# RMSNorm with SiLU on one core: other piece sizes in the first storing phase, and one alignment directive less

## The chip, the core and the metric

The kernel runs on one core of a Trainium2 chip. The core has engines that run side by side, each with its own list of instructions: VectorE (DVE in the profile), ScalarE (ACT), GpSimd (POOL), SyncE (SP) and TensorE (PE, unused here). Sixteen DMA engines move data between the memory of the chip (HBM) and the core's buffer SBUF. The metric is the device time of one execution in microseconds; lower is better.

## The reference

```python
x: 16 x 1024 x 512 float32; gamma: 512; eps
rms = np.sqrt(np.mean(x ** 2, axis=-1, keepdims=True) + eps)
x_norm = x / rms * gamma
return x_norm * (1.0 / (1.0 + np.exp(-x_norm)))
```

There are 16,384 rows of 512 elements. Each row is divided by the root of its mean square, multiplied by gamma, and passed through SiLU. Every byte is read once (33.55 MB) and written once (33.55 MB).

## The kernel before

**Tiles.** The 16,384 rows are spread over 128 partitions, so a partition has 128 rows. When this text says "row n" it means one row of every partition, 128 x 2 KB = 256 KB. The rows are cut into six groups in DRAM (L28), and inside a group each partition's rows are contiguous, so that a load or store of n rows is one run of n x 2 KB per partition. SBUF holds a ring of 96 rows (`xb`, L29): row 96 goes where row 0 was, and so on.

**Chunks.** The computation goes in 32 chunks of 4 rows (`cn`, L37). For chunk k, ScalarE squares the four rows; two of them are summed by its accumulator (L181) and two go to PSUM (L188), where VectorE adds them up (L234). GpSimd adds eps (L162) and raises to the power -0.5 (L169). VectorE multiplies each row by its factor and by gamma in place (L245). ScalarE applies SiLU in place (L200), two chunks behind its squares (L223 to L230).

**Loads.** SyncE issues all ten loads in order (L30, L31, function `load`, L118 to L127). The first two are placed in the entry block, ahead of the start barrier (L142 to L151). The first seven, rows 0 to 95, fill the ring and wait for nothing. Each of the last three, (96,16), (112,12) and (124,4), overwrites a part of the ring and so waits for each store that reads that part (`over`, L121); in addition the table `behind` (L35) lets (96,16) wait for one store more. A semaphore that SyncE has waited for once is not waited for again. SyncE does nothing between these waits, so a load behind a waiting load waits too.

**Stores.** ScalarE issues the eight stores (L32, L33, `store`, L206 to L212) in its own instruction list, between its squares and SiLUs. A store waits for the SiLU of its last chunk. The table `hold` (L34) keeps all stores back until chunk 12 and until load (64,28) has landed, and store (32,32) until chunk 22 and until load (112,12) has landed. Work on the DMA engines therefore falls into four phases: loading rows 0 to 95, storing rows 0 to 31 (the first storing phase), loading rows 96 to 127, and storing rows 32 to 127. The first storing phase has three stores, (0,16), (16,12) and (28,4), and ScalarE issues them one after the other.

**Semaphores.** Each DMA has a semaphore of its own, `ld[i]` or `st[u]`. Each of the 16 DMA engines adds one to it when its share is done; the waiting engine goes on at 16, that is, when the last DMA engine is done.

**Alignment.** For ScalarE, VectorE and GpSimd an `addr_align` is put ahead of the first instruction of the entry block (L131 to L141). It makes that engine's list begin at a chosen slot, counted within blocks of 128 instructions: slot 8, 40 and 0. It computes nothing. Instructions reach an engine through DMA transfers of their own, which the profile shows as queue q14. Loads are queue q1 and stores are queue q10. A list without the directive begins wherever the loader puts it.

Of the kernel before, what the change touches and what calls it, by code (L numbers as in the profile page):

```python
# [9 lines left out]
def kernel(  # L10
# [7 lines left out]
    nc = tc.nc  # L18
# [10 lines left out]
    ring = 96  # L29
    loads = [(0, 4), (4, 4), (8, 8), (16, 16), (32, 32), (64, 28)]  # L30
    loads += [(92, 4), (96, 16), (112, 12), (124, 4)]  # L31
    stores = [(0, 16), (16, 12), (28, 4), (32, 32), (64, 32)]  # L32
    stores += [(96, 16), (112, 8), (120, 8)]  # L33
    hold = {0: ((64, 28), 12), 3: ((112, 12), 22)}  # L34
    behind = {(96, 16): (16, 12)}  # L35
    early = 2
    cn = 4  # L37
    n_sq = 2
# [13 lines left out]
    behind = {loads.index(a): stores.index(b) for a, b in behind.items()}  # L52
# [78 lines left out]
    for queue, engine, offset in (  # L131
        (nc.scalar, mybir.EngineType.Activation, 8),
        (nc.vector, mybir.EngineType.DVE, 40),
        (nc.gpsimd, mybir.EngineType.Pool, 0),
    ):
        ins = queue.addr_align(128, offset=offset, max_nops=0).ins
        assert here[-1] is ins or here[-1].name == ins.name
        here.pop()
        entry.insert(
            next(i for i, other in enumerate(entry) if other.engine == engine), ins  # L140
        )  # L141
# [161 lines left out]
```

## Time and profile before

| what | value |
|---|---|
| median of 3 runs | 160.28 us (160.19 to 160.35) |
| the profiled execution: its own time | 160.17 us |
| the profiled execution: its span, first to last instruction | 159.3 us |
| VectorE busy | 124.4 us (78%) |
| ScalarE busy | 129.7 us (81%) |
| GpSimd busy | 65.4 us (41%) |
| HBM read and written | 33.56 MB and 33.56 MB, 421 GB/s over the span |

The span is what the trace covers; 0.9 us of the execution's own time lie around it. The page gives busy time by engine, then the span in 40 slices of 4 us. A digit is the busy share in tenths, and the DMA row is the mean over the 16 DMA engines. A view of one stretch of time counts packets: a packet is one contiguous run moved by one DMA engine, here mostly the rows of one partition in one load or store (8, 16, 24 or 32 KB and more), or the 4-byte increment of a semaphore. These views book a packet's bytes and busy time where the packet begins, so a share over a short stretch can exceed 100%. The trace also holds the start, length, queue and size of each packet.

### The profile page before, as it was taken

Reading aid. Unit: us, or ns where it says so; the run is one execution under the profiler, and the core shown is the slowest. Engines: PE = TensorE matmul, PEld = TensorE weight load, DVE = VectorE, ACT = ScalarE, POOL = GpSimd, SP = SyncE. Lnnn points to the kernel's source line nnn. Section 1 sums busy time; section 2 is a strip of 40 time slices with the busy share of each in tenths; the row PEclk is TensorE's granted clock in tenths of the full one; section 3 lists DMA queues with packets and bytes.
Section 4 is the critical chain, followed back from the end, with each engine's and each line's share of the span. In section 5 each row is a group of like instructions: output and inputs, shape, how many; then the busy total and the mean of one; then the engine's idle time right before and its main releaser. Section 6 shows DMA issues by size and latency. Waiting matters only on the chain.

```text
span 159.3 us, 503 instructions
## 1 busy us (share of the span) xinstructions
DVE 124.4 (78%) x162; ACT 129.7 (81%) x193; POOL 65.4 (41%) x71
## 2 busy tenths in 40 slices
DVE  0049996999289999599999999999999999992000
ACT  0675979997499995999999999999999999945000
POOL 1035553555145555155555555555555555540000
DMA  7999997998999969999899898969969969999997
GB/s 251 448 467 407 411 593 329 510 444 362 461 432 446 461 280 446 477 399 426 370 397 411 387 469 379 609 280 510 527 263 527 527 263 527 395 395 395 440 420 325
DMA packets 2750, 67.17 MB, mean 422 GB/s; under 512 B 437, under 2 KB 437, under 8 KB 441
## 3 DMA queue, kind: packets, MB, share of 16 engines
q1 hardware_dynamic: 1440, 33.56, 49.7%
q10 hardware_dynamic: 1304, 33.57, 49.0%
q14 instruction: 6, 0.04, 0.1%
HBM read 33.56 MB, written 33.56 MB: 421 GB/s over the span
## 4 chain that ended last, share of the span: by engine, by line
ACT 57%; DMA 25%; DVE 4%; issue 3%; ACTq 1%; SPq 0%
ACT xb L200 25%; DMA xb<-in_x_dram 25%; ACT junk L181 18%; ACT sq L188 14%; DVE xb L245 3%; ACTq L210 1%; DVE ms L234 1%; SPq L125 0%; ACTq L178 0%
## 5 line engine op out<-in xcount | busy, mean ns | idle before, releaser
L245 DVE SCALAR_TENSOR_TENSOR xb<-xb,rstd,gamma_sb 128x512 f32<-128x512 f32 x128 | 87.3, 744 | 0.0
L200 ACT ACTIVATE xb<-xb 128x2048 f32<-128x2048 f32 x32 | 60.9, 1903 | 5.0 <-DVE xb L245 3.4
L234 DVE TENSOR_REDUCE ms<-sq 128x2 f32<-128x1024 f32 x32 | 39.2, 1223 | 19.0 <-ACT sq L188 16.0
L162 POOL TENSOR_SCALAR aeps<-ms 128x4 f32<-128x4 f32 x32 | 20.6, 644 | 71.6 <-DVE ms L234 71.6
L169 POOL TENSOR_TENSOR rstd<-aeps,neg_half 128x4 f32<-128x4 f32 x32 | 44.0, 1376 | 2.7
L181 ACT ACTIVATE junk<-xb 128x512 f32<-128x512 f32 x64 | 37.2, 582 | 6.3 <-DMA xb<-in_x_dram 6.3
L188 ACT ACTIVATE sq<-xb 128x1024 f32<-128x1024 f32 x32 | 32.1, 1005 | 0.0
L181 ACT ACTIVATION_READ_ACCUMULATOR junk<-xb 128x1 f32 x64 | 11.9, 186 | 0.0
L221 ACT ACT_TABLE_LOAD x1 | 1.3, 1283 | 5.4 <-issue 5.4
L258 DVE LOAD_MASK_SELECT gamma_sb<-gamma x1 | 0.0, 14 | 1.1 <-DMA gamma<-in_gamma_dram 1.1
L258 DVE STREAM_SHUFFLE gamma_sb<-gamma 128x512 f32<-128x512 f32 x1 | 0.7, 716 | 0.0
L156 POOL MEMSET blank<- 128x16 f32 x1 | 0.1, 111 | 1.1 <-POOLq L66 1.1
L157 POOL MEMSET gamma<- 128x512 f32 x1 | 0.5, 524 | 0.0
L284 POOL MEMSET const-float32-0.0<- 128x1 f32 x1 | 0.1, 98 | 0.7 <-issue 0.7
L284 POOL MEMSET const-bfloat16-1.0<- 128x1 bf16 x1 | 0.1, 101 | 0.0
L284 POOL MEMSET const-uint8-127<- 128x1 uint8 x1 | 0.1, 101 | 0.0
L158 POOL MEMSET neg_half<- 128x4 f32 x1 | 0.1, 101 | 0.0
L284 POOL MEMSET const-float32-1.0<- 128x1 f32 x1 | 0.1, 99 | 0.0
## 6 DMA issues: line engine op xcount, KB each, us to landing
xb<-in_x_dram SPq DMA_DIRECT2D x2, 4096.0 KB, 16.3
out_dram<-xb ACTq DMA_DIRECT2D x2, 4096.0 KB, 15.3
xb<-in_x_dram SPq DMA_DIRECT2D x1, 7168.0 KB, 55.8
xb<-in_x_dram SPq DMA_DIRECT2D x4, 1024.0 KB, 13.6
out_dram<-xb ACTq DMA_DIRECT2D x2, 2048.0 KB, 13.7
out_dram<-xb ACTq DMA_DIRECT2D x1, 3072.0 KB, 19.6
xb<-in_x_dram SPq DMA_DIRECT2D x1, 3072.0 KB, 19.0
xb<-in_x_dram SPq DMA_DIRECT2D x1, 2048.0 KB, 11.1
```

The source lines that it names most:

```text
L157: nc.gpsimd.memset(gamma4, 0.0).then_inc(s_zero, 1)
L162: nc.gpsimd.tensor_scalar(out=aeps[:, k, :], in0=ms[:, k, :], scalar1=eps_f, scalar2=None, op0=ALU.add,),
L169: nc.gpsimd.tensor_tensor(out=rstd[:, k, :], in0=aeps[:, k, :], in1=neg_half, op=ALU.pow),
L181: acc = nc.scalar.activation(out=junk[n % 2], in_=xb[:, at + j, :], func=AF.Square, scale=inv_d**0.5, accum_out=ms[:, k, j : j + 1],)
L188: square = nc.scalar.activation(out=sq[k % 2], in_=xb[:, at : at + n_sq, :], func=AF.Square, scale=inv_d**0.5,)
L200: nc.scalar.activation(out=rows, in_=rows, func=AF.Silu), s_norm, k + 1
L210: nc.scalar.dma_start(out=dram(of, stores[t]), in_=buf(stores[t])),
L221: nc.scalar.preload_act_table_set("silu_and_others")
L234: nc.vector.tensor_reduce(out=ms[:, k, 0:n_sq], in_=sq[k % 2], op=ALU.add, axis=mybir.AxisListType.X,),
L245: ins = nc.vector.scalar_tensor_tensor(out=row, in0=row, scalar=rstd[:, k, j : j + 1], in1=gamma_sb, op0=ALU.mult, op1=ALU.mult,)
L258: nc.vector.stream_shuffle(gamma_sb, gamma4, [0] * 32), s_gld, 16
L284: nc = _bacc.Bacc("TRN2", target_bir_lowering=False, num_devices=1)
```

## The change

The first storing phase is cut into 16, 8 and 8 rows in place of 16, 12 and 4, and `behind` names the second of these, so that load (96,16) waits for stores (0,16) and (16,8). Load (112,12) goes into ring rows 16 to 27, which are now read by stores (16,8) and (24,8): SyncE waits for the third store ahead of this load, where it waited for the third store only ahead of load (124,4). ScalarE issues the three stores at the same place as before. GpSimd's list loses the alignment directive, and with it one instruction of its entry block; the lists of ScalarE and VectorE keep theirs and keep their lengths.

```diff
-    stores = [(0, 16), (16, 12), (28, 4), (32, 32), (64, 32)]
+    stores = [(0, 16), (16, 8), (24, 8), (32, 32), (64, 32)]
     stores += [(96, 16), (112, 8), (120, 8)]
     hold = {0: ((64, 28), 12), 3: ((112, 12), 22)}
-    behind = {(96, 16): (16, 12)}
+    behind = {(96, 16): (16, 8)}
...
     for queue, engine, offset in (
         (nc.scalar, mybir.EngineType.Activation, 8),
         (nc.vector, mybir.EngineType.DVE, 40),
-        (nc.gpsimd, mybir.EngineType.Pool, 0),
     ):
```

## The prediction

> **What bounds the kernel now.** I read the page first. Loads and stores together keep the 16 DMA engines busy for nearly the whole span:
>
> ```profile
> span 159.3 us, 503 instructions
> ...
> q1 hardware_dynamic: 1440, 33.56, 49.7%
> q10 hardware_dynamic: 1304, 33.57, 49.0%
> q14 instruction: 6, 0.04, 0.1%
> ```
>
> 49.7% and 49.0% make 98.7%, so about 2 us are lost per DMA engine, of which the packet list puts the first 1.0 us ahead of the first packet. VectorE (78%) and ScalarE (81%) have room. After the last SiLU at 146.4 us the stores already queued run on to 158.8 us, so the end is the end of the slowest DMA engine, and ScalarE's 57% in the chain is work beside full queues. The question is what each DMA engine loses at the change of phase. SyncE's waits name it:
>
> ```profile
> SPq L123 <- DMA out_dram<-xb: 74.8, 1, 74.8
> SPq L125 <- DMA out_dram<-xb: 1.3, 1, 1.3
> ```
>
> The 74.8 us are the wait before load (96,16); the 1.3 us are the wait for store (28,4) before load (124,4). The timeline of SyncE shows when the wait ended:
>
> ```profile
> 79.22 2.65 SPq L125 DMA_DIRECT2D xb<-in_x_dram  x3
> ```
>
> Store (16,12) landed at 79.13 us, the load was issued at 79.22 and its first packets begin at 80.18: 1.05 us from landing to packet. The DMA view of 79.72 to 80.16 us shows the hole between:
>
> ```profile
> DMA packets 6, 0.02 MB, mean 56 GB/s; under 512 B 3, under 2 KB 3, under 8 KB 3
> ...
> q10 hardware_dynamic: 6, 0.02, 13.5%
> ```
>
> Three data packets begin there and no load packet. By the packet list 11 of the 16 engines finish store (28,4) at 79.55 to 79.68 us, two at 79.74 and 79.86, and three late ones at 80.02, 80.98 and 81.08.
>
> **Who is late, and why that matters.** The late engines carry instruction fetches. In 2.6 to 3.2 us:
>
> ```profile
> q1 hardware_dynamic: 27, 0.22, 93.3%
> q14 instruction: 3, 0.02, 10.0%
> ```
>
> Each fetch takes 0.32 us, and the load packet behind it takes 0.68, 0.88 or 0.94 us in place of 0.31: three engines fall 0.7 to 0.95 us behind. One fetch more at 70.59 us (0.31, and the 24 KB packet behind it 1.37 for 0.91) and one at 78.64 (0.31, and 0.50 for 0.31) fall on two of these three. They are the engines that finish at 80.98 and 81.08.
>
> The hole costs a prompt engine about 0.6 us idle, plus a slow first load packet (1.69 to 2.21 us for 1.213). The two last engines lose nothing: their first load packets start at 80.98 and 81.08, take 1.24 and 1.21 us and end at 82.22 and 82.30. The prompt ones end theirs at 82.00 to **82.49**. So the hole levels the engines, and only 82.49 - 82.30 = **0.19 us** of it stands in the end time. The ends agree: all 16 finish within 158.30 to 158.77 us.
>
> **The change, part by part.**
>
> *Bytes and packets.* Before, an engine's share of rows 16 to 31 is 8 packets of 24 KB and 8 of 8 KB at steps of 0.908 and 0.305 us: 9.70 us. After, it is 16 of 16 KB at 0.607 us (steps of the last store): 9.71 us. The difference is 0. ScalarE issues three stores from 59.11 us as before: nothing.
>
> *Earlier release.* The engine last in store (16,12) begins it at 70.90 us and, with the fetch's 0.46 us, finishes at 78.62; landing is 0.5 us later. With 8 packets of 0.607 it finishes at 70.90 + 0.46 + 4.86 = 76.22, lands at 76.72, and loads begin at 77.77. Prompt engines begin store (24,8) at about 74.68 and end it at 79.54; the last two end it at 80.97 and 81.08 as now. Every engine then has a load queued before its stores run out: 1.8 us of cover on prompt engines (before: -0.6), 3.3 on the last. If no store packet is interleaved, prompt engines gain about 1.3 us each, but the last engine still begins its loads at 81.08. The end moves from the 82.49 group to the 82.30 engine: **-0.19 us**. Nothing later levels the engines again; prompt ones would end near 157.2.
>
> *The new wait.* Load (112,12) now waits for store (24,8), with (124,4) behind it on SyncE. A store that finishes at 81.08 lands at 81.6, and its load is on offer at 82.7, while (96,16) keeps the engines busy to 79.54 + 8 x 1.213 = 89.2 (prompt) and 90.8 (last). The cover is 6.5 us, so the cost is 0. If that cover went, each late microsecond would delay the end.
>
> *Interleaving.* No view of before shows 16 KB stores and 32 KB loads queued on one engine together. The nearest rows: ScalarE's scratch store (64-byte packets) is issued at 2.05 us and its first packet runs only at 5.65, behind loads, 2.7 us later than a store's usual 0.9 after issue would have it. From then on it alternates with load packets, one for one (5.6 to 6.6 us):
>
> ```profile
> q1 hardware_dynamic: 51, 0.41, 96.8%
> q10 hardware_dynamic: 47, 0.00, 3.2%
> ```
>
> Load packets keep their 0.31 us there, so one bound is 0 per alternation. The other is the extra on a packet behind a fetch, the only row where changing queues costs something: 0.19 to 0.63 us. Below nothing is excluded for a packet that already runs at 27 GB/s. I take 0: in the scratch row a newcomer waited for roughly eight packets of 8 KB, and prompt engines have only two or three store packets left at 77.77, the last five.
>
> The Trainium skill, "DMA: Bandwidth & Descriptors", section "Queues, rings and completion order", says that a DMA engine takes turns between queues, a packet each. That speaks against this change: by it the earlier load would take turns with store (24,8) and delay the semaphore on which load (112,12) now waits, which makes the first rival the forecast.
>
> *The directive.* GpSimd's list is 85 instructions with its entry block and 84 after. From slot 0 it stays within a block of 128; from an unknown slot it may cross a border, and a fetch then falls somewhere else. From the rows above a fetch costs one DMA engine 0.5 to 0.95 us, or gains as much where it goes. The last engines carry two fetches each; the third late one, 1.06 us ahead of the last, carries one. I take 0, since GpSimd's fetches presumably fall on that third engine. GpSimd's start has cover: the early loads occupy the queues to about 7 us, and SyncE passed the start barrier at 2.3.
>
> **Sum.** 160.17 - 0.19 = 159.98 us for the profiled execution. The median shown is 0.11 above it, so 160.28 - 0.19 = 160.09; I say **160.1 us**, own range 159.9 to 160.5.
>
> **Rivals.**
>
> *Slower: packets alternate and the new wait takes the place of the old.* At 78.04 the last engine has five store packets and the semaphore ahead. Taking turns with loads, it sends them after six loads: 78.04 + 5 x 0.607 + 6 x 1.213 = 88.35, landing 88.85, load (112,12) on offer at 89.9. Prompt engines are out of work at 78.32 + 2 x 0.607 + 8 x 1.213 = 89.24: the old hole again, ten microseconds later, levelling again at about the old cost. That alone is 0. Each of the 11 alternating packets that costs extra adds to the last engine: 0.19 each is 2.1 us, half of that 1.05, hence **161.3 us**, up to 162.4. It decides from 0.03 us per packet (0.33 us in all). For it: the strict alternation once scratch runs. Against it: no extra on the loads there. Chance 0.25.
>
> *Slower: a fetch of GpSimd falls late on an engine that is among the last.* Fetch 0.5 to 0.95 us, less what that engine had in hand: about **160.8 us**. For it: the start slot is unknown. Against it: the third engine has 1.06 us in hand when no levelling follows. Chance 0.10.
>
> *Faster: the last engines lose their lag.* If fetches move so that their lag shrinks to the third engine's, the end falls by 0.19 + 1.06 = 1.25, to about **159.0 us**. For it: lag is all that keeps the hole's 1.3 us from the end. Against it: VectorE's and ScalarE's lists keep slots and lengths. Chance 0.15.
>
> **How the numbers follow.** Forecast 0.50, rivals 0.25, 0.10, 0.15. A measurement here tells about 0.2% (0.32 us) from no change. Faster by more: the faster rival and the edge of the forecast, 0.15 + 0.05 = 0.20. Slower by more: most of the two slower rivals and the other edge, 0.31. Within: 0.49. The range reaches into both sides until about 2 in 10 are left out: 159.5 to 161.4.
>
> **What would show it.** Right: the SyncE wait ends near 76.8; no engine is idle between 77 and 82 us; the SyncE wait for store (24,8) ends by 83; final packets spread from about 157.2 to 158.6. Wrong: load and store packets mixed from 78 to 88 us with longer times, a SyncE wait near 88 and a new hole near 89.5 (first rival); a q14 packet after 85 us (second); two late engines less than 1 us behind (third).

## The result, and the profile after

The changed kernel takes 161.51 us (median of 9 runs, 160.78 to 161.96), the kernel before 160.22 us in the same comparison (160.15 to 160.44). The ratio is 1.0072, 95% interval 1.0059 to 1.0085: slower by 0.7% (the ratio is that of the means; the medians differ by 1.29 us). The forecast was 160.1 us in a range of 159.5 to 161.4; sign and size are both wrong, and the time lies just outside the range.

The page of the changed kernel, its span and its DMA queues (packets, MB, share of 16 engines):

```profile
span 160.2 us, 502 instructions
...
q10 hardware_dynamic: 1304, 33.57, 49.3%
q1 hardware_dynamic: 1440, 33.56, 49.0%
q14 instruction: 5, 0.04, 0.1%
```

The span grew by 0.9 us (159.28 to 160.21, unrounded). The execution's own time is 161.51 us, so 1.30 us lie outside the span, where 0.89 did before. Between the two profiled executions the loss of 1.34 us thus has two parts: 0.93 us inside the span and 0.41 us outside. They have different causes. The profiled execution is the median one. Two of the nine took only 160.78 and 160.81 us, with spans of 159.5 us: the loss inside the span is not there every time.

**Inside the span.** The release came as worked out. SyncE's waits in the changed kernel:

```profile
SPq L123 <- DMA out_dram<-xb: 72.2, 1, 72.2
SPq L125 <- DMA out_dram<-xb: 6.5, 1, 6.5
```

The first, ahead of load (96,16), is 2.6 us shorter than before and ends at 76.7 us; the second is the new wait for store (24,8). SyncE's timeline, from 70 and from 80 us on, shows when each ends:

```profile
76.73 7.61 SPq L125 DMA_DIRECT2D xb<-in_x_dram  x3
...
83.54 0.80 SPq L125 DMA_DIRECT2D xb<-in_x_dram  x2
```

Load (112,12) is issued at 83.54 us, 6 us before any DMA engine needs it. The new wait costs nothing.

The cost is in the first load packet of the DMA engine that is last. The DMA view of 81.04 to 81.24 us holds a single packet:

```profile
DMA packets 1, 0.03 MB, mean 164 GB/s; under 512 B 0, under 2 KB 0, under 8 KB 0
...
q1 hardware_dynamic: 1, 0.03, 67.2%
```

A packet's whole length is booked where it begins, so its length can be read from the share: 67.2% of 16 engines over 0.20 us is 2.15 us, for 32 KB. The same reading of the kernel before, 81.05 to 81.15 us, at the same place:

```profile
DMA packets 2, 0.03 MB, mean 328 GB/s; under 512 B 1, under 2 KB 1, under 8 KB 1
...
q1 hardware_dynamic: 1, 0.03, 75.8%
q10 hardware_dynamic: 1, 0.00, 0.6%
```

75.8% x 16 x 0.10 us = 1.21 us. The last engine begins its loads at the same moment in both kernels and pays 0.94 us more for the first packet in the new one. At the end of the changed kernel, this engine alone is still storing, from 158.78 to 159.8 us:

```profile
DMA packets 1, 0.02 MB, mean 16 GB/s; under 512 B 0, under 2 KB 0, under 8 KB 0
...
q10 hardware_dynamic: 1, 0.02, 3.7%
```

One data packet begins there (at 159.21 us, ending at 159.82); the other 15 engines end by 158.74. Before, all 16 ended within 158.30 to 158.77.

The packet lists give the sequence on an engine; I put a packet down to the engine whose packet before it ends within 10 ns of its start. S is a store packet, L a load packet, with start and length in us:

```
before, prompt   79.27 S 0.31 | idle 0.64   | 80.21 L 2.01 | 82.23 L 1.22
before, last     80.47 S 0.31 | 80.77 S 0.31 | 81.08 L 1.21 | 82.29 L 1.21
after, prompt    77.67 S 0.61 | 78.28 S 0.73 | 79.02 S 1.21 | 80.23 L 1.21 | 81.44 L 1.21
after, last      79.82 S 0.61 | 80.42 S 0.61 | 81.05 L 2.15 | 83.21 L 1.21
```

The hole is gone, but not its price. A prompt engine moves its last store packet at half rate (16 KB in 1.208 us for 0.61) and the one before it somewhat slowed, and loses about 0.7 us instead of 1.4. Across the idle stretch the rule cannot tell which load packet belongs to which engine, so the first row shows a typical pair. The last engine, which lost nothing before, loses 0.94. From 83.21 against 82.49 us before, a difference of 0.72, it is further behind at its end (1.05), mainly through the first packet of load (124,4), which took 0.67 us for 0.31. Landing after the last packet took 0.12 us less: 0.93.

What the prompt engines gain is taken back at the next change of phase, where store (32,32) is held until load (112,12) has landed on all engines. ScalarE's timeline in the changed kernel:

```profile
99.44 0.34 ACTq L209 DMA_DIRECT2D out_dram<-xb  x1
```

In the kernel before:

```profile
98.66 0.34 ACTq L210 DMA_DIRECT2D out_dram<-xb  x1
```

The last engine's lateness delays the issue by 0.78 us, and prompt engines, whose loads are done near 99.6 us, wait for it until 100.3.

**Outside the span.** GpSimd's first memset in the changed kernel:

```profile
0.23 0.10 POOL L283 MEMSET const-float32-0.0<- 128x1 f32 x1 [0.23 <-issue]
```

And in the kernel before:

```profile
0.66 0.10 POOL L284 MEMSET const-float32-0.0<- 128x1 f32 x1 [0.66 <-issue]
```

Without the directive it comes 0.43 us earlier, and the time outside the span is 0.41 us longer. First memset plus time outside is 1.55 us before and 1.53 after.

### The profile page after: what moved, and what is told of

Same layout as the page of the kernel before. It is cut to its first block, busy times and chain, and to the rows that moved or that the text cites. A ratio compares the mean times of both kernels' runs of the same rounds, so it can differ in the third digit from the quotient of the medians.

```text
span 160.2 us, 502 instructions
## 1 busy us (share of the span) xinstructions
DVE 124.4 (78%) x162; ACT 129.7 (81%) x193; POOL 65.4 (41%) x71
## 4 chain that ended last, share of the span: by engine, by line
ACT 57%; DMA 24%; DVE 4%; issue 3%; ACTq 2%; SPq 0%
ACT xb L199 25%; DMA xb<-in_x_dram 24%; ACT junk L180 18%; ACT sq L187 14%; DVE xb L244 3%; ACTq L209 2%; DVE ms L233 1%; SPq L125 0%; ACTq L177 0%
```

## Experiments

Each comparison has its own runs of the kernel before beside it; their medians moved from 160.18 to 160.46 us, so ratios within a comparison are what counts. "Outside" is the profiled execution's time less its span. Theory A is that there are two separate costs, the moment of the release and the directive; theory B that the directive alone explains the loss; theory C that the size of the pieces does.

### One half of the change at a time

Pieces and release only, directive kept:

```diff
-    stores = [(0, 16), (16, 12), (28, 4), (32, 32), (64, 32)]
+    stores = [(0, 16), (16, 8), (24, 8), (32, 32), (64, 32)]
-    behind = {(96, 16): (16, 12)}
+    behind = {(96, 16): (16, 8)}
```

> Pieces 16, 8, 8 with the earlier release, GpSimd's directive kept. Theory A (two separate costs): the pieces cost the 0.9 us that the span grew, because the DMA engine that was last pays about 0.9 us more on its first load packet; the directive costs the 0.4 us that grew outside the span. Then this is about 161.1 us, with 0.9 us outside the span as in the kernel before, and one DMA engine ends about 1 us after the others. Theory B (the directive alone): losing it moved GpSimd's instruction fetch to 80.3 us, and that disturbs the change of phase; then this is 160.0 to 160.3 us.

Measured: 161.15 us against 160.41, ratio 1.0041 (1.0027 to 1.0055). Span 160.27, outside 0.88 us; fetches at 70.7 and 78.6 us as before. The last engine's first load packet took 2.09 us, after 0.36 us idle, and ended at 83.55.

Directive only:

```diff
-        (nc.gpsimd, mybir.EngineType.Pool, 0),
```

> Pieces as before, only GpSimd's directive removed. Theory A: +0.4 us outside the span and nothing inside, 160.6 us, with GpSimd's fetch near 80 us on the third late DMA engine, whose lag has room. Theory B: 161.1 to 161.5 us, all of the loss, inside the span.

Measured: 160.69 us against 160.41, ratio 1.0014 (1.0005 to 1.0023). Span 159.44, outside 1.31 us. GpSimd's fetch is gone from the start (two q14 packets there instead of three) and comes at 80.0 us, on an engine that is not among the last, without a trace in the end time.

Both halves cost, each in its own place: B falls, and so does the idea that the fetch at 80 us disturbs the loads, as far as a run with the old release can tell. 0.74 and 0.28 us make 1.02, of the 1.29 measured together; the other 0.27 us are not accounted for, and the changed kernel alone spreads over 1.2 us (160.78 to 161.96).

### Is it the cut or the moment?

From here on GpSimd's directive is kept in every run.

Four pieces, released after 28 rows as before:

```diff
+    stores = [(0, 16), (16, 8), (24, 4), (28, 4), (32, 32), (64, 32)]
+    behind = {(96, 16): (24, 4)}
+    hold = {0: ((64, 28), 12), 4: ((112, 12), 22)}
```

> Four pieces of 16, 8, 4 and 4 rows, load (96,16) released by the third, so after 28 rows as in the kernel before and with 4 rows to cover it; directive kept. Theory A (what counts is how many rows are left when the loads come): no change, 160.1 to 160.4 us. Theory C (what counts is the size of the pieces or the number of stores): 161 us, as with 16, 8, 8.

Measured: 160.40 us against 160.41, ratio 0.9997 (0.9987 to 1.0007).

The last 4 rows in twice as many packets:

```diff
+    stores = [(0, 16), (16, 12), (28, 2), (30, 2), (32, 32), (64, 32)]
+    hold = {0: ((64, 28), 12), 4: ((112, 12), 22)}
```

> Pieces 16, 12, 2, 2, released after 28 rows as before: the bytes beside the loads are those of the kernel before, in twice as many packets (16 of 4 KB per DMA engine). If the number of queued store packets makes the last engine pay: 0.5 to 0.9 us more, 160.9 to 161.3 us. If the time of the release counts: 160.3 to 160.5 us.

Measured: 160.39 us against 160.46, ratio 1.0001 (0.9992 to 1.0010). The number of queued packets doesn't count at this moment of release.

Pieces 16, 8, 8, but released when the kernel before releases:

```diff
         stored_by_sync.add(u)
+        if i in behind:
+            nc.sync.wait_ge(s_sum, 17)
```

> Pieces 16, 8, 8 and the directive kept, but SyncE also waits, ahead of load (96,16), for VectorE's 17th reduction, which ends at 79.3 us: the loads are released when the kernel before releases them. Theory A (the time that the loads wait beside queued stores counts): back to 160.3 to 160.5 us, and the last DMA engine's first load packet takes 1.2 to 1.4 us. Theory C (the 8-row pieces count): 161.1 us as with pieces 16, 8, 8 alone.

Measured: 160.54 us against 160.46, ratio 1.0012 (1.0003 to 1.0021). SyncE went on at 79.67 us rather than near 79.3:

```profile
79.67 2.77 SPq L127 DMA_DIRECT2D xb<-in_x_dram  x3
```

The last engine's first load packet took 1.74 us, not the 1.2 to 1.4 expected. C falls: with the cut of the changed kernel and nearly the old release, 0.12% is left of the pieces' 0.41%, and the release was 0.4 us late.

Pieces 16, 8, 8, released at 78 us:

```diff
+            nc.sync.wait_ge(s_norm, 15)
```

> Pieces 16, 8, 8, directive kept, load (96,16) held until VectorE's 15th group of rows is done, at 78.0 us: the moment of release of pieces 16, 10, 6, with the cut of the changed kernel. Theory A (the moment of the release decides, and the last DMA engine pays 0.8 to 0.95 us more on its first load packet for any release well before 79 us): 161.1 to 161.4 us. Theory D (only a release at the landing of the second store pays): 160.4 us.

Measured: 161.61 us against 160.36, ratio 1.0073 (1.0054 to 1.0093). The release:

```profile
78.17 4.32 SPq L127 DMA_DIRECT2D xb<-in_x_dram  x3
```

This costs more than the release at 76.8 us. Theory D (only a release at the landing of the second store pays) falls.

Pieces 16, 10, 6:

```diff
+    stores = [(0, 16), (16, 10), (26, 6), (32, 32), (64, 32)]
+    behind = {(96, 16): (16, 10)}
```

> Pieces 16, 10, 6: loads released two rows later than in the changed kernel, two earlier than before; directive kept. Theory A: the loads come on offer near 78.9 us while the last DMA engine has about four 12 KB packets left; if the extra on its first load packet comes from any overlap of over a microsecond, the span grows by 0.9 again (161.1 us); if it grows with the overlap, by about half (160.6 us). Theory B: 160.0 to 160.3 us.

Measured: 161.40 us against 160.41, ratio 1.0055 (1.0036 to 1.0074). That is more than either form of theory A expected. Two late engines paid here: first load packets of 1.99 and 2.18 us, each begun 0.3 to 0.9 us after the engine's last store packet.

### The ends of the scale

No extra wait, released after 16 rows:

```diff
-    behind = {(96, 16): (16, 12)}
+    behind = {}
```

> Pieces 16, 12, 4 as before, no extra wait: load (96,16) is released by store (0,16) alone, with 16 rows of stores still queued; load (112,12) then waits for store (16,12). Theory A with a fixed price (each DMA engine pays 0.8 to 0.95 us once at the change of phase): 161.1 to 161.4 us. Theory A with a price per alternating packet: 162 us and more, since eight packets or more alternate. If the alternation holds back the stores on which (112,12) waits, there is a second hole as well, and the time is over 162.

Measured: 160.74 us against 160.46, ratio 1.0019 (1.0010 to 1.0028): cheaper than the releases at 76.8 and 78.2 us, which neither form of theory A had. The loads are issued at 72.10 us, but the first load packet runs only at 76.94. Around it a store packet of 24 KB is slowed on every engine (1.77 to 1.81 us for 0.91 on ten of them, 1.02 to 1.75 on the others), and stores and loads mix. Load (96,16) ends at 90.82 us on the last engine, earlier than before (90.96), but each engine has one to four packets of store (28,4) left when its part of this load is done, and they go between the later loads until 93.4 us. With these counted in, the engines have both pieces of work done between 90.31 and 91.25 us, against 90.54 to 90.96 before: the last one has lost 0.29 us of the 0.46 by which the span grew.

Released after all stores:

```diff
+    stores = [(0, 16), (16, 8), (24, 8), (32, 32), (64, 32)]
+    behind = {(96, 16): (24, 8)}
```

> Pieces 16, 8, 8, load (96,16) released by the third store, so with no store left: the hole at its full length, on every DMA engine. The last engine's stores end at 81.1, loads come on offer at 82.6 and the slow first packet ends near 84.8, against 82.5 in the kernel before: 162.5 us. If it is under 161.2, leaving the overlap out is the better choice and the forecast's price of the hole was wrong.

Measured: 162.64 us against 160.46, ratio 1.0141 (1.0127 to 1.0155). The hole at its full length costs 2.2 us; here the price of an idle stretch plus a slow first packet was worked out rightly.

Pieces 16, 13, 3:

```diff
+    stores = [(0, 16), (16, 13), (29, 3), (32, 32), (64, 32)]
+    behind = {(96, 16): (16, 13)}
```

> Pieces 16, 13, 3, directive kept: released about 0.45 us later than before, so that the loads come on offer about 0.45 us before the last DMA engine runs out. All engines' loads start 0.45 us later, the last engine's first packet is partly slow: 160.7 to 160.9 us. If 160.4 us or less, the release of the kernel before is not the best one.

Measured: 160.93 us against 160.24, ratio 1.0039 (1.0024 to 1.0054). The last engine's first load packet took 1.99 us, although its loads were on offer only about 0.25 us before its stores ran out.

Pieces 16, 11, 5:

```diff
+    stores = [(0, 16), (16, 11), (27, 5), (32, 32), (64, 32)]
+    behind = {(96, 16): (16, 11)}
```

> Pieces 16, 11, 5, directive kept: the release falls between that of 16, 10, 6 (78.2 us, +0.9 us) and of the kernel before (79.1 us). Loads come on offer about 1.4 us before the last DMA engine runs out of stores. If the price appears as soon as that lead is over about 1 us: 161.1 to 161.4 us. If it grows evenly with the lead: 160.7 us.

Measured: 160.34 us against 160.24, ratio 1.0008 (0.9986 to 1.0030), and neither expectation holds: ten times in two groups, four from 159.78 to 159.93 us and six from 160.28 to 161.12. In the profiled execution (160.76 us) two late engines began their loads at 81.02 and 81.21 us. The first took 1.21 us for its packet, the other 1.98.

Put in order of the moment when SyncE goes on:

| SyncE goes on, us | kernel | ratio to before |
|---|---|---|
| 72.1 | released after 16 rows | 1.0019 |
| 76.8 | 16, 8, 8 | 1.0041 |
| 78.2 | 16, 8, 8 held by a wait | 1.0073 |
| 78.3 | 16, 10, 6 | 1.0055 |
| 78.7 | 16, 11, 5 | 1.0008, two groups |
| 79.2 | before | 1 |
| 79.4 | 16, 8, 4, 4 and 16, 12, 2, 2 | 0.9997 and 1.0001 |
| 79.7 | 16, 8, 8 held by a wait | 1.0012 |
| 80.0 | 16, 13, 3 | 1.0039 |
| 81.8 | 16, 8, 8 after all stores | 1.0141 |

The packet lists of these profiles also answer how much the lead counts. By lead I mean the time from when the loads are on offer (0.96 us after SyncE goes on, as in the kernel before) until the engine's own stores end. The two engines that end their stores last, with the extra on the first load packet (its length less 1.21 us):

| kernel | second last engine: lead, extra, us | last engine: lead, extra, us |
|---|---|---|
| 16, 13, 3 | 0.08, 0.60 | 0.25, 0.78 |
| 16, 8, 8 held to 79.7 | 0.17, 0.82 | 0.55, 0.53 |
| 16, 8, 4, 4 | 0.73, 0.46 | 0.96, 0.12 |
| before, with two directives for GpSimd (further down) | 0.81, 0.35 | 0.91, 0.11 |
| before | 0.80, 0.03 | 0.90, 0 |
| 16, 11, 5 | 1.36, 0 | 1.54, 0.77 |
| 16, 8, 8 | 3.1, 0 | 3.3, 0.88, and 0.36 idle |
| changed kernel | 2.9, 0.04 | 3.3, 0.94 |

Up to a lead of about 0.9 us the extra falls, with scatter, from 0.6 to 0.8 us to almost nothing. Beyond it the last engine pays again, and the second last, with nearly the same lead, does not. These are single executions, so the lead alone does not decide.

### The two groups

Pieces 16, 11, 5 again, one execution:

> Pieces 16, 11, 5 once more, for a second profile. If its time is near 159.8 us, the last DMA engines' first load packets take 1.2 us and all engines end within 0.6 us; if it is near 161 us, at least one of them takes about 2 us and ends about 1 us after the others.

Measured: 161.42 us. The DMA view of 81.2 to 81.4 us shows the last engine's first load packet, 83.2% x 16 x 0.20 us = 2.66 us long:

```profile
DMA packets 1, 0.03 MB, mean 164 GB/s; under 512 B 0, under 2 KB 0, under 8 KB 0
...
q1 hardware_dynamic: 1, 0.03, 83.2%
```

The same pieces without ScalarE's directive, which moves its fetch from 78.6 to 47.1 and 126.7 us:

```diff
-        (nc.scalar, mybir.EngineType.Activation, 8),
```

> Pieces 16, 11, 5 and ScalarE's directive removed (GpSimd's kept), which takes ScalarE's fetch away from 78.6 us, so that one DMA engine less runs late. Pieces 16, 11, 5 gave times in two groups, 159.8 to 159.9 and 160.3 to 161.1 us. If each late engine by itself either pays the 0.8 to 0.9 us or not, fewer late engines give more executions near 159.8 us and a median under that of the kernel before: 159.9 us. If it is not the late engines: a median of 160.3 us and the same two groups.

Measured: 160.22 us against 160.18, ratio 1.0017 (0.9999 to 1.0036); ten times from 159.91 to 161.07. The spread stays and the median does not fall, so the gain hoped for from fewer late engines did not show. But the profiled execution took 159.92 us, at the low end, and here is its last engine, 81.0 to 81.1 us:

```profile
DMA packets 2, 0.03 MB, mean 328 GB/s; under 512 B 1, under 2 KB 1, under 8 KB 1
...
q1 hardware_dynamic: 1, 0.03, 75.8%
q10 hardware_dynamic: 1, 0.00, 0.6%
```

75.8% x 16 x 0.10 us = 1.21 us, no extra. Load (96,16) ends at 90.69 us on its last engine, against 92.38 in the profile of 161.42 us, and the spans differ by 1.5 us (159.03 and 160.53). So the forecast's picture, last engine unharmed and the end a little earlier than before, does occur. With pieces 16, 8, 8 it is not the usual case; the two short executions of the changed kernel, with spans of 159.5 us, come near it.

### Does the price need the lag?

ScalarE's and VectorE's lists begin at slot 0, so that their fetches come at 79.0 and 100 to 101.5 us:

```diff
-        (nc.scalar, mybir.EngineType.Activation, 8),
-        (nc.vector, mybir.EngineType.DVE, 40),
+        (nc.scalar, mybir.EngineType.Activation, 0),
+        (nc.vector, mybir.EngineType.DVE, 0),
```

> The kernel before with ScalarE's and VectorE's start slots moved from 8 and 40 to 0: their fetches at 78.6 and 70.6 us come later, to about 83 and 102 us, so that the last DMA engines are only 0.7 to 0.95 us behind at the change of phase. The hole then opens about 0.8 us earlier, but the two fetches fall on engines that nothing levels again: between 160.0 and 160.7 us. It is the base for the next run.

Measured: 160.75 us against 160.36, ratio 1.0034 (1.0013 to 1.0055), with a wide spread (160.41 to 161.87).

With pieces 16, 8, 8 as well:

> Pieces 16, 8, 8 with both start slots at 0, against the run before this one. If the last engine pays its 0.9 us however far it lags: 0.7 to 0.9 us over that run. If the price needs the lag of 1.5 us that the fetches give: within 0.2 us of that run.

Measured: 161.24 us against 160.36 for the kernel before, ratio 1.0057 (1.0036 to 1.0078), 160.66 to 161.82. That is 0.5 us over the run before it, between the two answers, and both kernels spread over more than a microsecond. No fetch came near 83 us, where one was expected; it came at 79.0. This pair decides nothing.

### What the directive is worth

ScalarE's directive removed, GpSimd's kept:

```diff
-        (nc.scalar, mybir.EngineType.Activation, 8),
```

> The kernel before without ScalarE's directive, GpSimd's kept. If the 0.4 us outside the span are tied to GpSimd's list, the time outside the span stays 0.9 us. If they are tied to any list that begins without the branch of its directive, it is 1.3 us. The span may change by up to 0.9 us, since ScalarE's fetches move.

Measured: 160.34 us against 160.36, ratio 0.9997 (0.9985 to 1.0008); outside 0.89 us. Of these two lists only GpSimd's matters for the time outside; VectorE's was not tried.

A second directive for GpSimd:

```diff
+        (nc.gpsimd, mybir.EngineType.Pool, 16),
         (nc.gpsimd, mybir.EngineType.Pool, 0),
```

> The kernel before with a second directive ahead of GpSimd's list (slot 0, then slot 16), so that GpSimd branches twice before its first memset. If the measured time begins with GpSimd's first instruction after the branch: the first memset comes at about 1.1 us of the span in place of 0.66, the time outside the span falls to about 0.5 us and the median by 0.4 us. If the directive saves the 0.4 us in another way: no change outside the span.

Measured: 160.21 us against 160.24, ratio 0.9998 (0.9989 to 1.0008). GpSimd's first memset:

```profile
0.81 0.10 POOL L285 MEMSET const-float32-0.0<- 128x1 f32 x1 [0.81 <-issue]
```

Outside is 0.73 us. The second directive moved the memset by 0.15 us only, not the 0.45 expected, but outside fell with it: memset plus outside is 1.54 us (1.55 with one directive, 1.54 with none). So the time outside the span follows GpSimd's first memset: the measured time behaves as if it began with GpSimd's first work, and the directive delays that while SyncE's first load already runs. Where the measurement really begins no run shows. No kernel tried beats the kernel before beyond the interval.

## Why the prediction was wrong

- *Bound.* Right: the end is that of the slowest DMA engine, and the hole lies where it was read.
- *Bytes and packets.* Right: pieces 16, 8, 4, 4 with the old release are 0.9997, and doubling the packets is 1.0001.
- *Earlier release.* Landing was foreseen at 76.72 us and SyncE's wait ended at 76.7; the last engine's stores were to end at 81.08 and ended at 81.04. **The step that failed is "the last engine still begins its loads at 81.08"**, with 82.30 us taken as the end of its first load packet. It began at 81.05 and ended at 83.21. I had taken from the two late engines of the kernel before that an engine with a load queued pays nothing for the change from stores to loads. They paid 0.03 us and nothing with the loads on offer 0.8 and 0.9 us ahead; at about the same lead two other kernels paid 0.11 to 0.46. With more lead the last engine paid 0.8 to 1.0 us in the profiles of 16, 8, 8 and 16, 10, 6, and nothing in the 159.92 us execution of 16, 11, 5 without ScalarE's directive. Two packets in one execution were no bound for another lead.
- *Prompt engines gain 1.3 us.* Half right: 0.65 us by the median end of load (96,16) (90.73 before, 90.08 after), since their last store packets run at half rate while the loads begin. Interleaving was priced at 0 from packets of 64 bytes, which say nothing about this.
- *"Nothing later levels the engines again."* Wrong: store (32,32) waits for load (112,12) on all engines. Prompt engines could not have ended near 157.2 us in any case.
- *The new wait costs 0.* Right in cost: it ended at 83.5 us, 6 us before the need. By 83 was foreseen; on the last engine the semaphore's packet ran only after the slow load packet, at 83.2 us, and not before it.
- *The directive costs 0.* Wrong by 0.28 us in the median when removed alone (0.42 in the profile's time outside the span). I had looked for its cost in the fetches, which did no harm (GpSimd's fell at 80.3 us on an engine that was not among the last), and not outside the span, where the profile shows nothing but a difference of two numbers.
- *Rivals.* The first put 161.3 us on alternation, close in size for another reason: packets of stores and loads did not mix between 78 and 88 us and no second hole near 89.5 came. In its clause that a packet may run longer when both queues are active it pointed at the right place. The other two did not occur.

What stays open is why the last DMA engine pays again for a lead of 1.5 to 3.3 us when it pays little or nothing at 0.9, and why the same kernel can do either. The runs show that it goes engine by engine: one late engine paid and the other did not in the same execution, in the changed kernel, in 16, 8, 8 and in 16, 11, 5. They do not show what inside the DMA engine decides.

## What to carry to other kernels

Where loads follow stores on busy DMA engines, starting the loads earlier removed the idle time of most engines here but not the price of the change itself, and the time follows the engine that ends last: look at that engine's packets, not at the mean. The release moment has to be tried: of those tried here none beat 79.2 us, there were losses on both sides, and 78.7 us was the same only within its wide spread. Split a difference in time into span and the rest before explaining it; a part outside the span has a cause that no busy time shows.

## What the runs showed of the hardware

The store packet ahead of a DMA engine's first load packet can move at half rate: 16 KB in 1.208 us for 0.61 on 12 of 16 engines of the changed kernel, 24 KB in about 1.8 for 0.91 on ten in the kernel released after 16 rows. On the last engine of the changed kernel it took its usual 0.61. A load released into full store queues had its first packet only 3.4 us after SyncE went on in the changed kernel, where every engine sent all its store packets first, and 4.8 us after it in the kernel released after 16 rows; it was 0.96 us in the kernel before, where most engines had run out of stores by then. In the kernel released after 16 rows, from 84.4 to 90 us, stores and loads alternate at full length, one for one on 14 engines and in pairs on two: loads of 1.21 us and stores of 0.31.

The Trainium skill, "DMA: Bandwidth & Descriptors", section "Queues, rings and completion order", has a DMA engine take turns between its queues. The alternation after 84.4 us in the kernel released after 16 rows agrees with it (1.21 and 0.31 us in turn); the late start and the half rate at the beginning are not in that rule, and in the changed kernel no engine took turns between store (24,8) and the loads at all.

An instruction fetch of 8 KB takes 0.31 us on one DMA engine and lengthens the packet behind it by 0.2 to 0.6 us. The Trainium skill, "Runtime: NRT & Kernel Launch", section "Instruction fetch mechanics", calls the cost of crossing a block mostly hidden. That holds for the fetching engine here (ScalarE, whose fetch runs at 78.64 us in the kernel before, is busy without a gap from 76 to 84 us); the DMA engine that carries the fetch falls behind by 0.5 to 0.95 us, and a kernel bound by DMA can end by that engine.
